# Hybrid encoder layer on one core: the convolution norm's means from split sums, its low parts one piece later, the ninth tile of values from a 64-wide operand, and the first weight load on ScalarE's queue

## The chip, the cores and the metric

One Trainium2 chip, one core. The metric is the time of one execution of the program in microseconds (us) on that core; smaller is better. The engines work side by side: TensorE (PE) multiplies matrices into PSUM, VectorE (DVE) and ScalarE (ACT) work element by element, GpSimd (POOL) does the same more slowly and issues some transfers, and SyncE (SP) issues most transfers (DMA).

## The reference

One layer of a streaming encoder in float32 for 1024 prompt frames and 32 frames of a running stream, 1056 rows (T) in all, D_MODEL 1024:

```python
p = x @ w_in                      # GLU pair | q | k | v | forget logits | branch gates
u = p[:, :512] * sigmoid(p[:, 512:1024])
y = conv_1d(u_ext, w_dw) + b_dw   # causal, depthwise, 31 taps, 512 channels
y = silu(layer_norm(y, ln_conv_g, ln_conv_b))      # norm over the 512 channels
y_conv = y @ w_conv_out
o = attention(q, k, v, cumsum(log_sigmoid(f)))     # 8 heads of 64, frame-causal
m = sigmoid(g_conv) * y_conv + sigmoid(g_attn) * (o @ w_attn_out)
x1 = layer_norm(alpha * x + m @ w_o)
x2 = layer_norm(alpha * x1 + relu(x1 @ w_up)**2 @ w_down)
```

Returned are x2, the new keys, values and forget logarithms, and the last convolution rows.

## The kernel before

Everything lies transposed: channels on the 128 partitions, frames along the free axis, in three chunks of 352 columns (`CH`). To keep float32 accuracy with the faster operand form fp32r, each operand is split in a high part (a copy to fp32r, made by ScalarE) and a low part (the operand minus the high part, made by VectorE), and a product is three products: high by high, high by low, low by high. `mm3` and `dense` write these; a group for eight row blocks of 128 has 24 products. A weight matrix comes in two halves (`W.load`), each of which is split (`W.split`) into `whi` and `wlo`.

The order of every engine's instructions is written out by the program: the class `Issue` keeps an estimated clock per engine, and background steps (generators) say with `yield` from when they may go on; `I.service()`, called between products, lets due steps issue. `yield (MARGIN, tiles)` means: not before these tiles have been ready for 3 us by that estimate. `I.flush()` issues all that is left of the background steps at once.

The first stage, in the order of TensorE's row:

- 19 warm-up products on constants (`keep_warm`), then the first GLU product (`glu`, kind b, tile 0, chunk 0), which takes its input as it comes: `x_stream` loads pieces `xr0`, `xr1`, ... of two row blocks each and the halves of the first weight matrices, and splits them. Between its products stand 5 and 2 more warm-up products.
- The other GLU products. Behind the third of tile 0 the background step `conv` begins: 31 multiply-adds on VectorE per channel tile (`ca0` to `ca3`).
- The values (`ps_v`): for two halves of the heads, nine tiles of frames. A tile is an operand of 128 frames against 260 columns of weights, 24 products. The ninth tile takes the last 128 frames, of which only the 32 of the running stream are used.
- q and k, then 16 tiles of branch gates (`gates`): three groups per tile, `g0_0`, `g0_1`, `g0_2`, `g1_0` and so on, each copied out of PSUM by ScalarE (`gt0_0`, ...) and stored. The first six tiles belong to this stage, where such products have eight PSUM buffers; then comes `I.flush()`. The other ten tiles fill gaps in the attention stage, where they have two buffers (`bbank`): `g6_2` needs the buffer of `g6_0`, hence the copy `gt6_0`.

Beside the gates the rest of `conv` runs, the norm over the 512 channels, in three column blocks of 362 (`CC`): `summed` adds the four channel tiles (`lns_m0`, ...); TensorE multiplies the sum with a matrix of 1/512 (`mean_c`), which gives the mean on all partitions (`ps_mu_c0`, ...), a float32 product; VectorE subtracts it, ScalarE squares, and the same gives the variance (`ps_var_c0`, ...); ScalarE takes the root and VectorE the reciprocal (`rstd_c0`, ...). Then twelve pieces (block c, tile j) follow. For a piece VectorE scales (here called y), ScalarE makes the sigmoid `csig`; one piece later VectorE multiplies with it (called z), ScalarE makes the high part `csh`, VectorE the low part `csl`, and both are stored. GpSimd clears buffers of the attention stage and issues the first head's loads when the memory of this stage is free.

Of the kernel before, what the change touches and what calls it, by code (L numbers as in the profile page):

```python
# [9 lines left out]
F32 = mybir.dt.float32  # L10
# [7 lines left out]
P = 128  # L18
# [249 lines left out]
def hybrid_layer(ctx: ExitStack, tc, io):  # L268
# [34 lines left out]
    act(tiny, eps, AF.Sigmoid)  # L303

    def par(name, j):
        return prm[:, PRM[name] + j:PRM[name] + j + 1]
# [17 lines left out]
    class Weights:  # L324
# [4 lines left out]
        def load(self):  # L329
            i = len(self.raw)  # L330
            held["raw"] += 1
            self.raw.append(ring.tile([P, RW // 2], F32, tag="raw", bufs=RAWB, name=f"raw{i}"))
            w = plan[i // 2]
            n = w.shape[1] // 2
            dma(self.raw[i][:, :n], w[:, i % 2 * n:(i % 2 + 1) * n])
# [157 lines left out]
    with pool("conv") as pv_, pool("a") as pa, pool("pa", space=PSUM) as psa:  # L493
# [6 lines left out]
        def x_stream():  # L500
            raw = []

            def issue():
                i = len(raw)
                if i < 4 * NCH:
                    r = pa.tile([P, 2, CH], F32, tag="xr", bufs=XB, name=f"xr{i}")
                    dma(r, io["x"][2 * (i % 4):2 * (i % 4) + 2, :, chunks[i // 4]].rearrange("k p t -> p k t"))
                    raw.append(r)

            W.load()  # L510
            issue()
            issue()
            W.load()
            for _ in range(XB - 2):
                issue()
                if len(raw) == 4:
                    W.load()
                    W.load()
            W.split()
            for i in range(4 * NCH):  # L520
                if i == 1:
                    W.split()
                    W.load()
                    W.load()
                yield [raw[i]]
                cs = chunks[i // 4]
                for n in range(2):
                    k = 2 * (i % 4) + n
                    act(xh[k][:, cs], raw[i][:, n, :], AF.Copy)
                    tt(xl[k][:, cs], raw[i][:, n, :], f32(xh[k][:, cs]), SUB)  # L530
                xin.append(i)
                for _ in range((0, 1, 1, 2)[i] if i < 4 else 1):
                    issue()
# [22 lines left out]
        mean_c = pv_.tile([P, P], F32, name="mean_c")  # L556
        nc.gpsimd.memset(mean_c, 1.0 / C_CONV)
# [26 lines left out]
        def glu(kind, j, c):  # L584
# [3 lines left out]
            if (kind, j, c) == ("b", 0, 0):  # L588

                terms = on_x(glu_w[kind, j], c)  # L590
                for k, (wh, _, h, l) in enumerate(terms):
                    mm(ps, wh, h, k == 0, False)
                    mm(ps, wh, l, False, False)
                    keep_warm({1: 5, 3: 2}.get(k, 0))
                    I.service()
# [17 lines left out]
        def conv():  # L613
# [11 lines left out]
            def summed(kind, c, src):  # L625
# [4 lines left out]
                return a  # L630
# [5 lines left out]
            for c in range(3):  # L636
                yield (MARGIN, [sums[c]])
                mu = bank(f"mu_c{c}")[:, :CC]
                mm(mu, mean_c, sums[c], True, True)
# [6 lines left out]
            for c in range(3):  # L646
                yield (MARGIN, [sums[c]])
                var = bank(f"var_c{c}")[:, :CC]
                mm(var, mean_c, sums[c], True, True)
# [6 lines left out]
            late = None  # L656
            for piece in pieces + [None]:
                yield ("dve", 1500)
                if piece:
# [4 lines left out]
                    act(sg, y, AF.Sigmoid, bias=par("lcb", j))  # L664
                if late:
# [3 lines left out]
                    act(hi, z, AF.Copy)  # L669
                    tt(lo, z, f32(hi), SUB)  # L670
# [70 lines left out]

        for half in range(2):
            ws = [W.take() for g in range(2)]
            for t in range(9):
                tk = slice(t * P, (t + 1) * P) if t < 8 else slice(T - P, T)
                ps = bank("v")[:, :VW]
                terms = []
                for k in range(KD):
                    wh, wl = (w[:, (k % 4) * VW:(k % 4 + 1) * VW] for w in ws[k // 4])
                    terms.append((xh[k][:, tk], xl[k][:, tk], wh, wl))  # L750
                dense(ps, terms)
                r = P if t < 8 else DEC
                ps = ps[P - r:P, :]
                v32 = pa.tile([P, 256], F32, tag="v32", bufs=2, name=f"v32_{half}_{t}")
                act(v32[:r], ps[:, 0:256], AF.Copy)
                act(zt[0:r, t, 4 * half:4 * half + 4], ps[:, 256:VW], AF.Copy)
# [1202 lines left out]
```

## Time and profile before

| | us |
|---|---|
| median of 3 runs | 1445.39 (1444.92 to 1445.43) |
| the profiled execution | 1445.13 |
| its span, first to last instruction | 1443.0 |
| TensorE busy | 1427.9 |
| VectorE busy | 1121.0 |
| ScalarE busy | 679.1 |

The profile is of one execution. A timeline row gives start, length, engine, source line, operation, output and inputs with shapes, and in brackets the idle time ahead of it and what ended it. Nearly all operations have the line of a helper, so tile names tell them apart, and the names come without numbers. Lengths of TensorE's products are those of one product through a pipeline and overlap; the pace is the distance of their starts.

### The profile page before, as it was taken

The page shows a single profiled execution, that of the slowest core. Times are in us where ns is not written, and L with a number is a line of the kernel's source. Part 1 is how long each engine was busy: PE and PEld are TensorE (multiplying, and loading weights), DVE is VectorE, ACT ScalarE, POOL GpSimd, SP SyncE. Part 2 cuts the span into 40 slices and gives each one's busy share as a digit, 9 for nine tenths or more (in the row PEclk, how much of TensorE's full clock was granted, in tenths as well). Part 3 has the DMA queues.
Part 4 walks back from the last instruction along what each step waited for, and adds up shares of the span by engine and source line. Part 5 has one row for each costly group of instructions (what it writes and reads, how often), then busy time and mean ns, then how long its engine had stood idle before and what let it go on. Part 6 is the DMA issues. An engine that isn't in the chain of part 4 may idle for free.

```text
span 1443.0 us, 28013 instructions
## 1 busy us (share of the span) xinstructions
PE 1427.9 (99%) x10643; PEld 1406.3 (97%) x10643; DVE 1121.0 (78%) x1927; ACT 679.1 (47%) x1426; POOL 124.5 (9%) x183
## 2 busy tenths in 40 slices
PE   9999999999999999999999999999999999999996
PEld 8999999999999999999999999999999999999996
DVE  6999899875666555756697888889876799889668
ACT  5113433455656556533245666676657323322134
POOL 0000000023455533000000000000000000000000
PEclk9999999999999999999999999999999999999998
DMA  7125454278455557425243348766689999894212
GB/s 247 48 61 160 159 171 167 85 244 233 120 150 147 155 146 260 152 93 182 85 138 120 131 152 295 249 241 230 228 283 342 340 321 330 270 324 179 67 45 77
DMA packets 157441, 267.91 MB, mean 186 GB/s; under 512 B 22680, under 2 KB 81272, under 8 KB 157308
## 3 DMA queue, kind: packets, MB, share of 16 engines
q1 hardware_dynamic: 156492, 264.24, 55.0%
q0 software_dynamic: 544, 1.59, 0.5%
q8 instruction: 84, 1.38, 0.4%
q14 instruction: 49, 0.40, 0.1%
q10 hardware_dynamic: 272, 0.29, 0.1%
HBM read 168.29 MB, written 97.74 MB: 184 GB/s over the span
## 4 chain that ended last, share of the span: by engine, by line
PE 97%; DVE 1%; ACT 0%; DMA 0%; issue 0%; SPq 0%; DVEq 0%
PE ps_u L206 18%; PE ps_d L206 17%; PE ps_g L206 13%; PE ps_o L206 6%; PE ps_dn L206 6%; PE ps_up L206 5%; PE ps_v L206 4%; PE ps_yc L206 3%; PE ps_k L206 3%; PE ps_glua L206 3%; PE ps_q L206 3%; PE ps_glub L206 3%; PE ps_yo L206 3%; PE ps_s L206 3%; PE ps_pv L206 2%; PE ps_tr L210 2%
## 5 line engine op out<-in xcount | busy, mean ns | idle before, releaser
L235 DVE SCALAR_TENSOR_TENSOR ca<-u,prm,ca 128x1086 f32<-128x1086 f32 x120 | 161.8, 1348 | 2.4
L206 PE MATMUL ps_g<-xh,whi 128*128 128x352 f32 x384 | 131.8, 343 | 0.0
L218 ACT ACTIVATE swhi<-s 128x512 fp32r<-128x512 f32 x100 | 61.9, 624 | 148.2 <-DVE s L227 139.8
L206 PE MATMUL ps_g<-xh,wlo 128*128 128x352 f32 x384 | 123.8, 322 | 0.0
L206 PE MATMUL ps_g<-xl,whi 128*128 128x352 f32 x384 | 121.5, 322 | 0.0
L206 PE MATMUL ps_u<-tl,swhi 128*128 128x264 f32 x416 | 118.4, 285 | 0.0
L206 PE MATMUL ps_u<-th,swhi 128*128 128x264 f32 x416 | 118.2, 284 | 0.0
L206 PE MATMUL ps_u<-th,swlo 128*128 128x264 f32 x416 | 118.2, 284 | 0.0
L218 ACT ACTIVATE whi<-raw 128x512 fp32r<-128x512 f32 (+1 forms) x120 | 69.7, 624 | 68.6 <-PE ps_glua L206 21.8
L227 DVE TENSOR_TENSOR tl<-ps_tr,th 128x512 fp32r<-128x512 f32 (+2 forms) x96 | 51.5, 553 | 60.1 <-ACT th L218 59.4
L206 PE MATMUL ps_d<-hu_h,swhi 128*128 128x264 f32 x480 | 93.0, 285 | 0.0
L206 PE MATMUL ps_d<-hu_l,swhi 128*128 128x264 f32 x480 | 92.8, 285 | 0.0
L218 ACT ACTIVATE r<-r 128x528 f32<-128x528 f32 (+1 forms) x120 | 73.9, 615 | 37.8 <-DVE r L227 35.5
L227 DVE TENSOR_TENSOR r<-r,ps_u 128x528 f32<-128x528 f32 x91 | 62.7, 701 | 29.5 <-PE ps_u L206 29.5
L227 DVE TENSOR_TENSOR wlo<-raw,whi 128x512 fp32r<-128x512 f32 (+1 forms) x100 | 64.9, 687 | 23.5 <-ACT whi L218 21.6
L206 PEld LDWEIGHTS ps_u<-th,swhi 128*128 128x128 f32 x416 | 78.3, 188 | 0.0
L206 PEld LDWEIGHTS ps_u<-th,swlo 128*128 128x128 f32 x416 | 78.3, 188 | 0.0
L206 PEld LDWEIGHTS ps_u<-tl,swhi 128*128 128x128 f32 x416 | 78.2, 188 | 0.0
L227 POOL TENSOR_TENSOR acc<-acc,lnrest 128x288 f32<-128x288 f32 x4 | 3.0, 796 | 856.7 <-ACT lnrest L218 856.7
L206 PEld LDWEIGHTS ps_d<-hu_h,swhi 128*128 128x128 f32 x480 | 74.6, 189 | 0.3 <-issue 0.2
L206 PEld LDWEIGHTS ps_d<-hu_l,swhi 128*128 128x128 f32 x480 | 74.6, 189 | 0.0
L206 PEld LDWEIGHTS ps_g<-xh,whi 128*128 128x128 f32 x384 | 72.7, 189 | 0.8
(424 smaller groups left out, 5005.5 us busy)
## 6 DMA issues: line engine op xcount, KB each, us to landing
h_s<-sp SPq DMA_DIRECT2D x84, 528.0 KB
raw<-in_w_in_dram SPq DMA_DIRECT2D x64, 256.0 KB
hu_h<-h_s SPq DMA_DIRECT2D x30, 528.0 KB
hu_l<-h_s SPq DMA_DIRECT2D x30, 528.0 KB
sraw<-in_w_up_dram SPq DMA_DIRECT2D x52, 256.0 KB
hu<-h_s SPq DMA_DIRECT2D x24, 528.0 KB
sraw<-in_w_ds_dram SPq DMA_DIRECT2D x48, 256.0 KB
g_s<-gt SPq DMA_DIRECT2D x48, 176.0 KB
```

Of the source, the lines that this page charges most:

```text
L206: self.nc.tensor.matmul(ps, lhsT=w, rhs=x, start=start, stop=stop)
L210: self.nc.tensor.transpose(ps, x, ident)
L218: self.nc.scalar.activation(out, in_, func, **kw)
L227: (self.nc.vector if eng == "dve" else self.nc.gpsimd).tensor_tensor(out, a, b, op)
L235: self.nc.vector.scalar_tensor_tensor(out, a, s, b, op0, op1)
```

## The change

Four edits. **(a)** `x_stream`: the first half of the first weight matrix is loaded through ScalarE's queue instead of SP's, and ScalarE's first table load and `tiny` stand behind that issue; the second half is split behind the second input piece instead of the first; the first GLU product has 2 and 1 warm-up products inside it instead of 5 and 2. **(b)** `summed` splits each sum of the norm in a high part (`csh_m0`, ...) and a low part (`csl_m0`, ...), `mean_c` is fp32r, and a mean is two fp32r products instead of one float32 product. **(c)** The low part of a piece and its stores are written one piece later, behind the next piece's z. **(d)** The ninth tile of values: ScalarE copies the 32 columns of each high and each low part side by side into `xs`, an operand 64 wide, which is multiplied with the high and the low weights, 16 products per half; rows 0 to 31 and 32 to 63 of the result are copied out and added by VectorE. (The product of the two low parts comes along; it was left out before.)

```diff
-    act(tiny, eps, AF.Sigmoid)
...
-        def load(self):
+        def load(self, queue=None):
...
-            dma(self.raw[i][:, :n], w[:, i % 2 * n:(i % 2 + 1) * n])
+            dma(self.raw[i][:, :n], w[:, i % 2 * n:(i % 2 + 1) * n], queue)
...
-            W.load()
+            W.load(nc.scalar)
+            act(tiny, eps, AF.Sigmoid)
...
-                if i == 1:
+                if i == 2:
                     W.split()
...
-        mean_c = pv_.tile([P, P], F32, name="mean_c")
-        nc.gpsimd.memset(mean_c, 1.0 / C_CONV)
+        mean_c = pv_.tile([P, P], F32R, name="mean_c")
+        nc.gpsimd.memset(f32(mean_c), 1.0 / C_CONV)
...
-                    keep_warm({1: 5, 3: 2}.get(k, 0))
+                    keep_warm({1: 2, 3: 1}.get(k, 0))
...
-                return a
+                parts = [pv_.tile([P, CC], F32R, tag=x, bufs=4, name=f"{x}_{kind}{c}") for x in ("csh", "csl")]
+                act(parts[0], a, AF.Copy)
+                tt(parts[1], a, f32(parts[0]), SUB)
+                return parts
...
-                yield (MARGIN, [sums[c]])
+                yield (MARGIN, sums[c])
...
-                mm(mu, mean_c, sums[c], True, True)
+                for i, a in enumerate(sums[c]):
+                    mm(mu, mean_c, a, i == 0, i == 1)
...
-                mm(var, mean_c, sums[c], True, True)
+                for i, a in enumerate(sums[c]):
+                    mm(var, mean_c, a, i == 0, i == 1)
...
-            late = None
-            for piece in pieces + [None]:
+            late = last = None
+            for piece in pieces + [None, None]:
...
+                before, last = last, None
...
                     act(hi, z, AF.Copy)
+                    last = c, j, z, hi, lo
+                if before:
+                    c, j, z, hi, lo = before
                     tt(lo, z, f32(hi), SUB)
...
+        xs = pa.tile([P, 2, CH], F32R, tag="xr", bufs=XB, name="xs").rearrange("p a x -> p (a x)")
+        xs = xs[:, :2 * KD * DEC].rearrange("p (k x) -> p k x", k=KD)
+        for k in range(KD):
+            for i, t in enumerate((xh, xl)):
+                act(xs[:, k, i * DEC:(i + 1) * DEC], f32(t[k][:, SEQ:T]), AF.Copy)
...
-                dense(ps, terms)
+                if t < 8:
+                    dense(ps, terms)
+                else:
+                    for n, (x, *w2) in enumerate(terms):
+                        for i, w in enumerate(w2):
+                            mm(ps[0:2 * DEC], x, w, n == i == 0, n == KD - 1 and i == 1)
+                        I.service()
...
+                    for i in range(2):
+                        act(both[i], ps[i * DEC:(i + 1) * DEC], AF.Copy)
+                    tt(both[0], both[0], both[1], ADD)
+                    ps = both[0]
```

The estimates of `Issue` move other instructions with these. In TensorE's row the first product of a mean goes from the middle of the group `g2_0` into `g2_2`, the last variance from `g3_0` into `g4_1`. The PSUM buffer of `g6_0` is one whose last reader was the copy `gt3_1`, and is now one whose last reader is `gt5_2`; `g6_2` waits for `gt6_0` in both. Behind the last piece the order of TensorE, VectorE and ScalarE is the same before and after.

ScalarE at the end of the first stage, before, from the copy of the stage's last gate product (`gt5_2`) to the copy of the next stage's first (`gt6_0`); the numbers in `csig2_3` are block and tile:

```order
L218 ACTIVATE gt5_2_3515<-ps_g5_2_94_3478 128x352
L218 ACTIVATE whi29_3518<-raw58_3250 128x512
L218 ACTIVATE whi29_3518<-raw59_3254 128x512
L218 ACTIVATE csig2_3_3529<-ca3_261,prm_131 128x362
L218 ACTIVATE csh2_2_3532<-ca2_260 128x362
L218 ACTIVATE csh2_3_3541<-ca3_261 128x362
L218 ACT_TABLE_LOAD
L218 ACTIVATE tiny_134<-eps_132 128x1
L218 ACTIVATE gt6_0_3617<-ps_g6_0_3592 128x352
```

The same place after the change, from `gt5_2` on; `csh2_2`, `csh2_3`, the table load, `tiny` and `gt6_0` come behind the last row shown:

```order
L218 ACTIVATE gt5_2_3503<-ps_g5_2_94_3468 128x352
L218 ACTIVATE whi29_3506<-raw58_3254 128x512
L218 ACTIVATE whi29_3506<-raw59_3258 128x512
L218 ACTIVATE csig1_3_3517<-ca3_261,prm_131 128x362
L218 ACTIVATE csh1_2_3520<-ca2_260 128x362
L218 ACTIVATE csig2_0_3527<-ca0_258,prm_131 128x362
L218 ACTIVATE csh1_3_3530<-ca3_261 128x362
L218 ACTIVATE csig2_1_3537<-ca1_259,prm_131 128x362
L218 ACTIVATE csh2_0_3540<-ca0_258 128x362
L218 ACTIVATE csig2_2_3547<-ca2_260,prm_131 128x362
L218 ACTIVATE csh2_1_3550<-ca1_259 128x362
L218 ACTIVATE csig2_3_3559<-ca3_261,prm_131 128x362
```

Behind `gt5_2` one sigmoid and two high parts stood ahead of `gt6_0`, and now five sigmoids and six high parts do.

VectorE from the split of weight matrix 29 (behind `gt5_2` in both) to the end of the norm, before:

```order
L227 TENSOR_TENSOR wlo29_3519<-raw58_3250,whi29_3518 128x512
L227 TENSOR_TENSOR wlo29_3519<-raw59_3254,whi29_3518 128x512
L235 SCALAR_TENSOR_TENSOR ca3_261<-ca3_261,prm_131,rstd_c2_3153 128x362
L235 SCALAR_TENSOR_TENSOR ca2_260<-ca2_260,prm_131,csig2_2_3486 128x362
L227 TENSOR_TENSOR csl2_2_3533<-ca2_260,csh2_2_3532 128x362
L235 SCALAR_TENSOR_TENSOR ca3_261<-ca3_261,prm_131,csig2_3_3529 128x362
L227 TENSOR_TENSOR csl2_3_3542<-ca3_261,csh2_3_3541 128x362
```

The same after the change, up to the low part of piece (1,3); behind it the operations of block 2 go on in the same turn, up to the low part of piece (2,3):

```order
L227 TENSOR_TENSOR wlo29_3507<-raw58_3254,whi29_3506 128x512
L227 TENSOR_TENSOR wlo29_3507<-raw59_3258,whi29_3506 128x512
L235 SCALAR_TENSOR_TENSOR ca3_261<-ca3_261,prm_131,rstd_c1_3233 128x362
L235 SCALAR_TENSOR_TENSOR ca2_260<-ca2_260,prm_131,csig1_2_3482 128x362
L227 TENSOR_TENSOR csl1_1_3486<-ca1_259,csh1_1_3485 128x362
L235 SCALAR_TENSOR_TENSOR ca0_258<-ca0_258,prm_131,rstd_c2_3298 128x362
L235 SCALAR_TENSOR_TENSOR ca3_261<-ca3_261,prm_131,csig1_3_3517 128x362
L227 TENSOR_TENSOR csl1_2_3521<-ca2_260,csh1_2_3520 128x362
L235 SCALAR_TENSOR_TENSOR ca1_259<-ca1_259,prm_131,rstd_c2_3298 128x362
L235 SCALAR_TENSOR_TENSOR ca0_258<-ca0_258,prm_131,csig2_0_3527 128x362
L227 TENSOR_TENSOR csl1_3_3531<-ca3_261,csh1_3_3530 128x362
```

The low part stands one piece later, and behind the weight's split begin the operations of piece (1,3) instead of (2,3).

ScalarE at the start of the program, before, up to the high part of the fourth row block:

```order
L218 ACT_TABLE_LOAD
L218 ACTIVATE tiny_134<-eps_132 128x1
L218 ACTIVATE whi0_210<-raw0_186 128x512
L218 ACTIVATE xh0_139<-xr0_188 128x352
L218 ACTIVATE xh1_140<-xr0_188 128x352
L218 ACTIVATE whi0_210<-raw1_192 128x512
L218 ACTIVATE xh2_141<-xr1_190 128x352
L218 ACTIVATE xh3_142<-xr1_190 128x352
```

The same after the change:

```order
L201 DMA raw0_185<-in_w_in_dram 128x512
L218 ACT_TABLE_LOAD
L218 ACTIVATE tiny_134<-eps_132 128x1
L218 ACTIVATE whi0_210<-raw0_185 128x512
L218 ACTIVATE xh0_138<-xr0_188 128x352
L218 ACTIVATE xh1_139<-xr0_188 128x352
L218 ACTIVATE xh2_140<-xr1_190 128x352
L218 ACTIVATE xh3_141<-xr1_190 128x352
L218 ACTIVATE whi0_210<-raw1_192 128x512
```

The load of `raw0` is issued here, and the split of `raw1` stands behind the two parts of `xr1`; VectorE's low parts follow the same order.

## Rows read from the trace of the kernel before

**Rows 1.** Parts 1 and 4 of the page, the whole span: busy time of an engine, its share of the span and its instructions; the last line is the chain of work that ended last, by engine.

```profile
PE 1427.9 (99%) x10643; PEld 1406.3 (97%) x10643; DVE 1121.0 (78%) x1927; ACT 679.1 (47%) x1426; POOL 124.5 (9%) x183
...
PE 97%; DVE 1%; ACT 0%; DMA 0%; issue 0%; SPq 0%; DVEq 0%
```

**Rows 2.** The chain that ended last, in order of time, between 240 and 340 us: start, length (us), engine, tile and number of instructions. `ps_g` are the gate products, `ps_mu_c` and `ps_var_c` the products with the matrix of means in the norm of the convolution.

```profile
245.34 24.91 PE ps_g L206 x156
270.25 0.61 PE ps_mu_c L206 x2
...
286.44 48.03 PE ps_g L206 x300
```

**Rows 3.** The same chain over the whole span: the product of the values (`ps_v`, 18 tiles of 24 products of 260 columns).

```profile
100.71 51.65 PE ps_v L206 x432
```

**Rows 4.** Timeline of VectorE (DVE) at the end of the norm of the convolution: start, length, instruction, and in brackets how long the engine had been idle before it and who released it. `csl` is the low part, `wlo` the low part of a weight matrix; the two SCALAR_TENSOR_TENSOR are the piece's scaling (written y in this text, its input is `rstd_c`) and the product with its sigmoid (written z, its input is `csig`).

```profile
313.28 0.54 DVE L227 TENSOR_TENSOR csl<-ca,csh 128x362 fp32r<-128x362 f32 x1 [0.62 <-ACT csh L218]
...
315.44 0.54 DVE L227 TENSOR_TENSOR csl<-ca,csh 128x362 fp32r<-128x362 f32 x1 [0.61 <-ACT csh L218]
...
319.14 1.30 DVE L227 TENSOR_TENSOR wlo<-raw,whi 128x512 fp32r<-128x512 f32 x2 [0.99 <-DMA g_s<-gt]
320.36 0.59 DVE L235 SCALAR_TENSOR_TENSOR ca<-ca,prm,rstd_c 128x362 f32<-128x362 f32 x1
320.86 0.59 DVE L235 SCALAR_TENSOR_TENSOR ca<-ca,prm,csig 128x362 f32<-128x362 f32 x1
322.07 0.54 DVE L227 TENSOR_TENSOR csl<-ca,csh 128x362 fp32r<-128x362 f32 x1 [0.61 <-ACT csh L218]
322.52 0.59 DVE L235 SCALAR_TENSOR_TENSOR ca<-ca,prm,csig 128x362 f32<-128x362 f32 x1
```

**Rows 5.** Timeline of ScalarE (ACT): one root of the norm, and then the stretch of rows 4. `gt` is the copy of a gate product out of PSUM; the one at 318.12 is `gt5_2`, the one at 325.08 `gt6_0`. `csh` is the high part of a piece, `whi` that of a weight matrix.

```profile
282.01 0.56 ACT L218 ACTIVATE rstd_c<-ps_var_c,eps 128x362 f32<-128x362 f32 x1
...
318.12 0.46 ACT L218 ACTIVATE gt<-ps_g 128x352 f32<-128x352 f32 x1 [0.54 <-PE ps_g L206]
318.49 1.15 ACT L218 ACTIVATE whi<-raw 128x512 fp32r<-128x512 f32 x2
321.54 0.49 ACT L218 ACTIVATE csh<-ca 128x362 fp32r<-128x362 f32 x1
323.15 0.51 ACT L218 ACTIVATE csh<-ca 128x362 fp32r<-128x362 f32 x1 [1.11 <-DVE ca L235]
323.67 1.28 ACT L218 ACT_TABLE_LOAD   x1
325.08 0.45 ACT L218 ACTIVATE gt<-ps_g 128x352 f32<-128x352 f32 x1
```

**Rows 6.** Timeline of TensorE (PE): the last product of the gate group `ps_g6_1`, and the first of `ps_g6_2` behind it.

```profile
325.39 0.32 PE L206 MATMUL ps_g<-xh,wlo 128*128 128x352 f32 x1
325.57 0.43 PE L206 MATMUL ps_g<-xh,whi 128*128 128x352 f32 x1
```

**Rows 7.** Timeline of VectorE in the norm of the convolution, from the first mean on: one column block's four subtractions, the start of its sum of squares, the next block's subtractions, later the three reciprocals and the first two pieces.

```profile
270.89 1.86 DVE L227 TENSOR_TENSOR ca<-ca,ps_mu_c 128x362 f32<-128x362 f32 x4 [0.15 <-PE ps_mu_c L206]
272.67 0.53 DVE L227 TENSOR_TENSOR lns_v<-sq_c,sq_c 128x362 f32<-128x362 f32 x1
274.39 1.85 DVE L227 TENSOR_TENSOR ca<-ca,ps_mu_c 128x362 f32<-128x362 f32 x4
...
284.69 6.96 DVE L239 RECIPROCAL rstd_c<-rstd_c 128x362 f32<-128x362 f32 x3
291.56 1.01 DVE L235 SCALAR_TENSOR_TENSOR ca<-ca,prm,rstd_c 128x362 f32<-128x362 f32 x2
```

**Rows 8.** Timeline of the first 11 us: TensorE's warm-up products (`ps_warm`, first 19, later 5 whose weight loads are shown), the split of the second half of the first weight matrix on ScalarE and VectorE with the idle time before it, and the six low parts of the input behind it on VectorE.

```profile
1.19 4.11 PE L542 MATMUL ps_warm<-warm 128*128 128x256 bf16 x19 [1.19 <-DVE warm L537]
...
6.88 0.44 PEld L542 LDWEIGHTS <-warm 128*128 128x128 bf16 x5
6.88 0.63 ACT L218 ACTIVATE whi<-raw 128x512 fp32r<-128x512 f32 x1 [0.93 <-DMA raw<-in_w_in_dram]
...
7.54 0.69 DVE L227 TENSOR_TENSOR wlo<-raw,whi 128x512 fp32r<-128x512 f32 x1 [0.98 <-ACT whi L218]
...
8.15 2.70 DVE L227 TENSOR_TENSOR xl<-xr,xh 128x352 fp32r<-128x352 f32 x6
```

**Rows 9.** Stretches at the start: from and to (us), length, busy us and instructions of each engine, then granted TensorE clock (1.00 is 2.4 GHz), DMA share and GB/s.

```profile
2.00:3.00 1.00, 1.00 (x7) 0.73 (x5) 0.00 (x0) 0.22 (x2) 0.00 (x0) 1.00 0.69 205
...
4.00:5.00 1.00, 1.00 (x6) 0.69 (x5) 0.40 (x1) 0.57 (x1) 0.00 (x0) 1.00 0.99 338
```

**Rows 10.** The same view at the end of the program, where TensorE has done its last product.

```profile
1430.00:1432.00 2.00, 1.70 (x7) 0.98 (x6) 0.63 (x3) 1.01 (x3) 0.40 (x1) 1.00 0.23 82
...
1434.00:1436.00 2.00, 0.00 (x0) 0.00 (x0) 1.97 (x3) 0.19 (x1) 0.65 (x1) 0.81 0.00 0
1436.00:1438.00 2.00, 0.00 (x0) 0.00 (x0) 2.00 (x7) 2.00 (x5) 0.00 (x0) 0.50 0.05 17
```

**Rows 11.** Timeline of GpSimd (POOL): it clears a buffer of the first head when the last variance product is done, then issues that head's loads (the last of them at 293.23).

```profile
286.56 1.00 POOL L827 MEMSET k<- 64x1088 f32 x1 [284.84 <-PE ps_var_c L206]
...
293.23 0.61 POOL L201 DMA_DIRECT2D q<-c_s  x1
```

More of the change, by code (lines that the diff above doesn't have):

```diff
@@ L646, in conv @@
             for c in range(3):
-                yield (MARGIN, [sums[c]])
+                yield (MARGIN, sums[c])
                 var = bank(f"var_c{c}")[:, :CC]
-                mm(var, mean_c, sums[c], True, True)
+                for i, a in enumerate(sums[c]):
+                    mm(var, mean_c, a, i == 0, i == 1)
                 rstds.append(pv_.tile([P, CC], F32, tag="lnrstd", bufs=3, name=f"rstd_c{c}"))
@@ L744, in hybrid_layer @@
             for t in range(9):
-                tk = slice(t * P, (t + 1) * P) if t < 8 else slice(T - P, T)
+                tk = slice(t * P, (t + 1) * P)
                 ps = bank("v")[:, :VW]
@@ L749, in hybrid_layer @@
                     wh, wl = (w[:, (k % 4) * VW:(k % 4 + 1) * VW] for w in ws[k // 4])
-                    terms.append((xh[k][:, tk], xl[k][:, tk], wh, wl))
-                dense(ps, terms)
+                    terms.append((xh[k][:, tk], xl[k][:, tk], wh, wl) if t < 8 else (xs[:, k, :], wh, wl))
                 r = P if t < 8 else DEC
-                ps = ps[P - r:P, :]
+                if t < 8:
[5 more added lines that the diff above has]
+                        I.service()
+                    both = pa.tile([P, 2, CH], F32, tag="xr", bufs=XB, name=f"xs_{half}")
+                    both = [both[:DEC, i, :VW] for i in range(2)]
+                    for i in range(2):
+                        act(both[i], ps[i * DEC:(i + 1) * DEC], AF.Copy)
+                    tt(both[0], both[0], both[1], ADD)
+                    ps = both[0]
                 v32 = pa.tile([P, 256], F32, tag="v32", bufs=2, name=f"v32_{half}_{t}")
-                act(v32[:r], ps[:, 0:256], AF.Copy)
-                act(zt[0:r, t, 4 * half:4 * half + 4], ps[:, 256:VW], AF.Copy)
+                act(v32[:r], ps[0:r, 0:256], AF.Copy)
+                act(zt[0:r, t, 4 * half:4 * half + 4], ps[0:r, 256:VW], AF.Copy)
                 vs = pa.tile([P, 4, P], F32R, tag="vs", bufs=2, name=f"vs_{half}_{t}")
```

## Prediction

> **What bounds the kernel now.** I read the page first: TensorE is busy for 99% of the span, and the chain that ended last is 97% TensorE [rows 1]. So an edit gains what it takes off TensorE's row of products, and loses what TensorE has to wait for. Next I read the chain in order of time around the norm of the convolution, to see what each product with the means costs there [rows 2], and the product of the values [rows 3]. Then I looked for the places where TensorE has no slack against the other engines. One stands right behind the norm. The third gate product behind the stage, `g6_2`, needs the PSUM buffer that ScalarE empties with the copy `gt6_0`, since the attention stage has two buffers for such products. That copy stands on ScalarE behind the whole rest of the norm: the last high part, a table load, then `gt6_0`, done at 325.53 [rows 5]. TensorE's last product of `g6_1` starts at 325.39 and the first of `g6_2` at 325.57 [rows 6], 0.18 us later, where the products of this stretch follow each other every 0.16 us (48.03 us for 300, rows 2). TensorE arrives there within 0.02 us of the moment when the buffer comes free. Any lengthening of the norm's tail behind `gt5_2` is therefore paid by TensorE in full.
>
> **Means as two fp32r products.** Before, each of six products takes 0.61 us from the row [rows 2]: 3.66 us. After, there are twelve fp32r products of 362 columns; the trace has the form with 352 columns at 0.160 [rows 2], so 0.165 each, 12 × 0.165 = 1.98. That gives back 1.7 us. Bounds: 0.16 each makes it 1.75; if each change of operand form cost another 0.05, 1.4. The six splits add six copies on ScalarE and six subtractions on VectorE, which has 22% of its time free [rows 1]; they hide, except for what they do to the tail, below.
>
> **Ninth tile in two products.** Two halves lose 24 − 16 = 8 products each. 51.65 us for 432 [rows 3] is 0.120 per product, so 16 × 0.120 = 1.9 us. The stationary operand is now 64 wide instead of 128; no row shows that form. If it made the remaining 32 products half as long, 32 × 0.06 = 1.9 more would come back; if the gain were eaten by something in that form, 0. I take 1.9, because the moving columns stay 260 and these set the pace in rows 3. ScalarE's 16 small copies ahead and four more copies behind lie beside products with eight PSUM buffers to spare; without that cover they would cost some 3 us.
>
> **First load by ScalarE, its second half one piece later, four warm-up products fewer.** TensorE is waiting for data in the first 11 us. What holds it is VectorE's row of low parts: it idles 0.98 us for the second half of the first weight matrix, which ScalarE idles 0.93 us for, and only then come the weight's low part and six input parts, 2.70 us long [rows 8]. In the new order the two input parts stand first, and their data are on the same queue ahead of that half (256 KB, at 338 GB/s [rows 9] about 0.75 us earlier). So most of the 0.98 us of idle time goes; I take 0.5, from 0 (later input pieces arrive no sooner) to 0.98. The load's issue on ScalarE I count at nothing: from 4 us on the transfers run at 338 GB/s with the DMA engines 0.99 busy, and only the stretch from 2 to 3 us has room (205 GB/s) [rows 9]. The Trainium skill, "DMA: Bandwidth & Descriptors", section on issuing engines, says that spreading transfers over issuing engines gives no bandwidth, only issue time; the busy share in rows 9 agrees, and by that rule the sum stays as it is. If a second queue did fill the room from 2 to 3 us (338 − 205 GB/s, 133 KB), all data would come up to 0.4 us earlier and the sum would be 1446.1. The warm-up products removed lie in TensorE's waits, so they count zero.
>
> **Low parts one piece later, and where the whole norm goes.** The edit removes VectorE's wait of 0.61 us per piece [rows 4]; a piece then takes its three operations, 0.50 + 0.51 + 0.45 = 1.46 us, instead of 2.16 (315.44 − 313.28). That alone shortens the tail. But the splits of the sums put each mean product later in TensorE's row: the first from the third gate tile's first group to its third, the last variance from the first group of the fourth tile into the second group of the fifth. So more of the norm is left when TensorE issues its last product ahead of the attention stage, and ScalarE's order shows it: behind `gt5_2` stood one piece's sigmoid and two high parts, now five sigmoids and six high parts, all ahead of the table load and `gt6_0`.
>
> Count from the start of the copy `gt5_2`. Now: VectorE splits the weight, starts y at +2.24 (320.36 − 318.12), and `gt6_0` ends at +7.41 (325.53 − 318.12) [rows 4, 5]. After the change y also starts at +2.24, but of piece (1,3), with four more pieces behind it. Five rounds of three operations at 1.46 bring VectorE to the last z at +9.55 (ScalarE needs about 1.1 per piece, so it keeps up). From the start of that z to the end of `gt6_0` it takes 325.53 − 322.52 = 3.01 now [rows 4, 5], so `gt6_0` ends at +12.55.
>
> TensorE has two groups of 24 products between, 48 × 0.160 = 7.7 us. And there is a second, smaller wait: the buffer of `g6_0` itself is now one that `gt5_2` empties (before, one that was free long ahead), so `g6_0` waits for that copy too. Both together: lag of `gt5_2` behind TensorE's last product of that group, plus 12.55, minus 7.7. For the lag I added up both engines from the first mean on. TensorE: 234 gate products × 0.160 + 12 × 0.165 = 39.4 us to the end of `g5_2`. VectorE: three blocks of 3.5 us (274.39 − 270.89, rows 7) plus 1.15 each for the new split (0.61 of wait and 0.54 of work, as a low part now has in rows 4), 14.0; three weight splits 3.7; the reciprocals 6.9 [rows 7]; eighteen piece operations at 0.49, 8.8; a wait of some 3.6 ahead of the third weight split, because ScalarE has a high part, a table load of 1.28, two roots and three gate copies to do first [rows 5]; about 2.5 of smaller waits and starts. That is 39.5, and ScalarE reaches `gt5_2` 0.2 to 1.5 us behind TensorE; I take 0.6. The new wait is 0.6 + 12.55 − 7.7 = 5.5 us, of which 4.4 stand in one piece ahead of `g6_2`. Bounds 4.9 and 7 (upper: stores of the pieces queue on SP behind two weight loads and a gate load, and a buffer of high parts comes free late).
>
> Behind this VectorE and ScalarE have the attention's first products to serve, and the order there is unchanged, so the 5.5 us are not won back. The first head's loads wait for the last variance product [rows 11], which comes about 13 us later; they are needed at 286.44 + 48.03 = 334.5 [rows 2], 41 us after the last issue at 293.23, so they stay hidden.
>
> **The sum.** −1.7 − 1.9 − 0.5 + 5.5 = +1.4 us. The profiled execution took 1445.13, 0.26 below the median of the runs shown: 1445.13 + 1.4 = **1446.5**. The forecast's own range is 1445.2 to 1448.8.
>
> **Rivals.** (1) The clock falls in the new wait: slower. At the end of the program TensorE is done at 1431.7 (1.70 us of work in that stretch), and the granted clock goes from 1.00 to 0.50 inside 1434 to 1436, where its mean is 0.81, so at 1435.2: 3.5 us after the last product [rows 10]. The wait ahead of `g6_2` is 4.4. [...] Price: at the start 19 warm-up products take 4.11 us, 0.216 each, where five later ones follow each other every 0.11 [rows 8]; so TensorE runs at the low level (1.2 GHz) for at least 4.1 us and loses 2.1. Time: 1446.5 + 2.1 = 1448.6. The Trainium skill, "TensorE: Matmul & The Clock Gate", Part 1, has the half-rate clock as the default that returns once TensorE is idle and is lifted by sustained work; rows 8 and 10 agree, and by that rule the sum is 1448.6 instead of 1446.5.
>
> (2) The tail does not hold TensorE: ScalarE and VectorE run further ahead than my count, or the rounds overlap better, so that `gt6_0` is as early as now. For it speaks that the change removes 0.61 us of wait per piece; against it the order of ScalarE, in which sixteen piece operations of VectorE lie between the weight split and `gt6_0`. Time: 1445.13 − 4.1 = 1441.0.
>
> (3) With four warm-up products fewer the clock rises later at the start, or falls again in the waits between the first products: a loss as in (1), 1448.6. Against it: the 19 products ahead are untouched and the gaps are under 1 us.
>
> **How the numbers follow.** About what a measurement of this kernel can tell from no change is 0.2%, 2.9 us: from 1442.5 to 1448.3. Chances: forecast 0.56 (0.03 of it slower, the rest within); clock falls 0.28 (0.04 within, 0.24 slower); tail doesn't hold 0.09 (faster); start clock 0.04 and late buffers beyond my bound 0.03 (slower). That makes faster 0.09, same 0.57, slower 0.34. The range leaves out most of (2) and the worst of (1): 1442.8 to 1450.0.
>
> **What would show it.** TensorE idle ahead of `g6_2`, released by ScalarE's `gt`: 4.4 us if right, none if (2). Ahead of `g6_0` about 1 us. `gt6_0` ending 12.5 us after `gt5_2` starts. Mean products 0.33 a pair; 432 − 16 = 416 products of values, in 49.7 us. VectorE's waits for `csh` gone in the pieces. Granted clock below 1.00 for a few us behind the wait would show (1), below 1.00 or products at 0.31 us after 8 us would show (3). Wrong altogether I would be if `g6_2` waited for nothing: then the change is a plain gain of 4 us.

## The result and the profile after

The changed kernel takes 1450.4 us, the median of 7 runs (1449.47 to 1451.03), against 1445.43 us for the kernel before (7 runs, 1444.92 to 1445.86): 1.0032 times the time, 95% interval 1.0022 to 1.0041. It is slower by more than the 0.2% that was taken as the bound, and 0.4 us above the range. The profiled execution took 1449.47 us with a span of 1447.2, so the pair of profiles differs by 4.2 us of span.

What each edit takes off TensorE came back as forecast. The chain that ended last, of the changed kernel (start, length, engine, tile, instructions):

```profile
12.22 3.85 PE ps_glua L206 x24
...
100.34 49.71 PE ps_v L206 x416
...
274.64 0.33 PE ps_mu_c L206 x2
...
327.07 10.47 PE ps_g L206 x54
...
657.94 47.20 PE ps_o L206 x390
...
1432.62 1.47 PE ps_md_last L206 x6
```

and the rows of the same view of the kernel before that stand against the first and the last two:

```profile
12.60 3.85 PE ps_glua L206 x24
...
654.59 47.20 PE ps_o L206 x390
...
1429.27 1.47 PE ps_md_last L206 x6
```

The start is 0.38 us earlier, the values take 49.71 instead of 51.65 us [rows 3], and a mean takes 0.33 instead of 0.61 [rows 2]. The loss stands in one place. TensorE's timeline behind the norm of the convolution, with the idle time in brackets:

```profile
313.78 0.32 PE L206 MATMUL ps_g<-xh,wlo 128*128 128x352 f32 x1
315.02 0.43 PE L206 MATMUL ps_g<-xh,whi 128*128 128x352 f32 x1 [0.92 <-ACT gt L218]
...
322.60 0.32 PE L206 MATMUL ps_g<-xh,wlo 128*128 128x352 f32 x1
327.07 0.43 PE L206 MATMUL ps_g<-xh,whi 128*128 128x352 f32 x1 [4.15 <-ACT gt L218]
...
328.14 0.39 PE L206 MATMUL ps_g<-xh,whi 128*128 128x352 f32 x1
328.34 0.49 PE L206 MATMUL ps_g<-xl,whi 128*128 128x352 f32 x1
328.63 0.49 PE L206 MATMUL ps_g<-xh,wlo 128*128 128x352 f32 x1
```

These are the two waits of the forecast: `g6_0` at 315.02, `g6_2` at 327.07, where the kernel before had none [rows 6]. From 328.3 us on the products follow each other every 0.29 us instead of 0.16. The granted clock of the same stretch (from and to, length, busy us and instructions of PE, PEld, DVE, ACT and POOL, granted clock, DMA share, GB/s):

```profile
327.00:328.00 1.00, 0.93 (x6) 0.93 (x7) 0.00 (x0) 0.37 (x2) 0.88 (x4) 1.00 0.58 175
328.00:329.00 1.00, 1.00 (x6) 1.00 (x6) 0.00 (x0) 0.00 (x0) 0.00 (x0) 0.63 0.58 174
329.00:330.00 1.00, 1.00 (x5) 1.00 (x4) 0.00 (x0) 0.00 (x0) 0.00 (x0) 0.50 0.60 176
330.00:331.00 1.00, 1.00 (x6) 1.00 (x5) 0.00 (x0) 0.00 (x0) 0.00 (x0) 0.50 1.00 85
331.00:332.00 1.00, 1.00 (x6) 1.00 (x6) 0.00 (x0) 0.00 (x0) 0.00 (x0) 0.67 0.65 66
332.00:333.00 1.00, 1.00 (x8) 1.00 (x7) 0.00 (x0) 0.00 (x0) 0.00 (x0) 1.00 0.80 277
```

So the clock went to its low level (1.2 GHz) for some 3.4 us, 1.2 us after TensorE had taken up work again. The 54 products of that stretch take 10.47 us; at 0.160 they would take 8.64: 1.83 us lost.

Who holds `g6_2` shows in ScalarE's timeline; `gt5_2` is the copy at 314.52, `gt6_0` and `gt6_1` are the two at 326.57, `gt6_2` the one at 334.98:

```profile
314.52 0.45 ACT L218 ACTIVATE gt<-ps_g 128x352 f32<-128x352 f32 x1
...
324.64 0.51 ACT L218 ACTIVATE csh<-ca 128x362 fp32r<-128x362 f32 x1 [0.31 <-DVE ca L235]
325.17 1.28 ACT L218 ACT_TABLE_LOAD   x1
...
326.57 0.80 ACT L218 ACTIVATE gt<-ps_g 128x352 f32<-128x352 f32 x2
334.98 0.47 ACT L218 ACTIVATE gt<-ps_g 128x352 f32<-128x352 f32 x1 [7.61 <-DMA g_s<-gt]
```

and ScalarE follows VectorE, whose pieces come in rounds of 1.46 us (318.19 − 316.73) up to the last z at 324.02:

```profile
316.73 0.59 DVE L235 SCALAR_TENSOR_TENSOR ca<-ca,prm,rstd_c 128x362 f32<-128x362 f32 x1
...
318.19 0.59 DVE L235 SCALAR_TENSOR_TENSOR ca<-ca,prm,rstd_c 128x362 f32<-128x362 f32 x1
...
324.02 0.59 DVE L235 SCALAR_TENSOR_TENSOR ca<-ca,prm,csig 128x362 f32<-128x362 f32 x1
```

The last row of ScalarE points at something the forecast had not looked at: `gt6_2` waits 7.61 us for the landing of `gt6_0`'s store, since the attention stage has two buffers for such copies. The kernel before has that wait too, 6.02 us long; in neither does TensorE wait for it. The experiments come back to it. The row of the kernel before:

```profile
332.24 0.47 ACT L218 ACTIVATE gt<-ps_g 128x352 f32<-128x352 f32 x1 [6.02 <-DMA g_s<-gt]
```

Why so much of the norm is left behind `gt5_2`: VectorE's reciprocals, with which the pieces begin, start at 295.18 instead of 284.69 [rows 7]. The six splits stand in VectorE's row, each with a wait of 0.57 to 0.63 us for the high part; its last low part of a sum is ready at 290.60, and then it idles 3.37 us for the split of a weight. TensorE's last product with the means comes at 295.38, 4.8 us behind its operand, since the planner asks for 3000 ns by its own count. VectorE's timeline there:

```profile
290.06 0.54 DVE L227 TENSOR_TENSOR csl_v<-lns_v,csh_v 128x362 fp32r<-128x362 f32 x1 [0.57 <-ACT csh_v L218]
293.97 1.29 DVE L227 TENSOR_TENSOR wlo<-raw,whi 128x512 fp32r<-128x512 f32 x2 [3.37 <-ACT whi L218]
295.18 6.96 DVE L239 RECIPROCAL rstd_c<-rstd_c 128x362 f32<-128x362 f32 x3
```

### The profile page after: what moved, and what is told of

Its sections match the earlier page's. It is cut to its first block, busy times and chain, and to the rows that moved or that the text cites. A ratio compares the mean times of both kernels' runs of the same rounds, so it can differ in the third digit from the quotient of the medians.

```text
span 1447.2 us, 28010 instructions
## 1 busy us (share of the span) xinstructions
PE 1425.8 (99%) x10623; PEld 1405.3 (97%) x10623; DVE 1122.8 (78%) x1935; ACT 685.5 (47%) x1452; POOL 124.2 (9%) x183
## 4 chain that ended last, share of the span: by engine, by line
PE 96%; DVE 2%; DMA 1%; ACT 1%; issue 0%; SPq 0%; DVEq 0%
PE ps_u L206 18%; PE ps_d L206 17%; PE ps_g L206 12%; PE ps_o L206 6%; PE ps_dn L206 6%; PE ps_up L206 5%; PE ps_v L206 3%; PE ps_yc L206 3%; PE ps_k L206 3%; PE ps_glua L206 3%; PE ps_q L206 3%; PE ps_glub L206 3%; PE ps_yo L206 3%; PE ps_s L206 3%; PE ps_pv L206 2%; PE ps_tr L210 2%
```

## The experiments

All were timed beside the kernel before on the same chip (its medians there are 1445.47 to 1445.74). The table has, from each trace, TensorE's waits for a gate copy (gt), the stretch with the low clock, the first product of the attention's scores, the first product of the up projection's long stage (`ps_u`), that of the last norm (`ps_md_last`) and what lies from there to the end of the span (to 0.05 us, as the span is read to 0.1), and the median and ratio of the timed runs.

| kernel | waits for gt | low clock | scores | ps_u | md_last | to the end | median us | ratio (95%) |
|---|---|---|---|---|---|---|---|---|
| before | none | none | 334.31 | 820.75 | 1429.11 | 13.89 | 1445.43 | |
| after | 0.92, 4.15 | 328 to 332 | 337.38 | 824.09 | 1432.46 | 14.74 | 1450.40 | 1.0032 (1.0022–1.0041) |
| e1_no_means | none | none | 329.85 | 818.83 | 1428.15 | 13.95 | 1444.13 | 0.9989 (0.998–0.9997) |
| e2_only_means | 1.52, 7.67 | 329 to 339 | 344.79 | 831.20 | 1439.73 | 13.87 | 1456.43 | 1.0071 (1.0057–1.0085) |
| e3_margin500 | 0.65, 2.53 | 334 to 341 | 336.34 | 826.41 | 1434.84 | 14.96 | 1449.42 | 1.0024 (1.0015–1.0033) |
| e4_busy | 0.55, 1.43, 0.75 | none | 337.33 | 824.26 | 1432.61 | 14.89 | 1449.92 | 1.0025 (1.0014–1.0035) |
| e5_margin_queue | 1.97 | none | 332.79 | 819.47 | 1428.09 | 14.91 | 1445.53 | 1.0001 (0.9992–1.001) |
| e6_busy_queue | 0.56, 1.25 | none | 336.33 | 822.80 | 1432.09 | 14.61 | 1447.97 | 1.0017 (1.0008–1.0026) |
| e7_start_ninth | 0.78 | none | 333.15 | 821.13 | 1429.51 | 13.89 | 1445.65 | 0.9999 (0.999–1.0007) |
| e8_only_late | none | none | 330.72 | 824.70 | 1433.16 | 14.24 | 1450.95 | 1.0036 (1.0022–1.005) |
| e9_pool_queue | none | none | 330.33 | 816.86 | 1425.21 | 13.89 | 1441.54 | 0.997 (0.996–0.9981) |
| e10_pool | none | none | 330.73 | 818.64 | 1428.72 | 13.88 | 1441.17 | 0.997 (0.9958–0.9981) |
| e11_margin1000 | 2.10, 2.72 | 334 to 341 | 336.64 | 825.12 | 1433.49 | 15.41 | 1448.62 | 1.0019 (1.001–1.0028) |

**Which edit makes the waits.** In e1 the means are fp32 products of whole sums again, in the changed kernel (`mean_c` is float32 again too; the products with `var` change in the same way):

```diff
-                parts = [pv_.tile([P, CC], F32R, tag=x, bufs=4, name=f"{x}_{kind}{c}") for x in ("csh", "csl")]
-                act(parts[0], a, AF.Copy)
-                tt(parts[1], a, f32(parts[0]), SUB)
-                return parts
+                return [a]
...
-                for i, a in enumerate(sums[c]):
-                    mm(mu, mean_c, a, i == 0, i == 1)
+                mm(mu, mean_c, sums[c][0], True, True)
```

> The changed kernel with the means of the norm as fp32 products of whole sums again (the start, the late low parts and the ninth tile stay). Theory T (the sums' split pushes the last variance product, and with it the norm's tail, behind gt5_2): ScalarE's order now has no piece of the norm between gt5_2 and gt6_0, so TensorE waits for nothing ahead of g6_0 and g6_2 and the granted clock stays 1.00 around 330 us; 1445.4 - 0.4 (start) - 1.9 (ninth tile) = 1443.1 us. Rival R (the extra round of the low parts and the stores that it shifts on SP hold TensorE): the waits of 0.9 and 4.1 us stay, the time is 1450.4 + 1.7 = 1452.

In e2 this edit stands alone in the kernel before.

> The kernel before with the split sums and fp32r means alone. Theory T: the same five sigmoids and six high parts stand between gt5_2 and gt6_0, and each piece takes 2.16 us instead of 1.46, so the tail is some 3.5 us longer than in the changed kernel and the wait ahead of g6_2 is 7 to 8 us; with the fall of the clock (1.8) and the 1.7 us that the means give back the time is 1445.4 - 1.7 + 9 + 1.8 = 1454.5 us. Rival R: no wait, the means give back 1.7 us: 1443.7.

Both went by theory T: no wait and a clock of 1.00 in e1, two waits in e2, TensorE's timeline:

```profile
317.80 0.43 PE L206 MATMUL ps_g<-xh,whi 128*128 128x352 f32 x1 [1.52 <-ACT gt L218]
333.38 0.66 PE L206 MATMUL ps_g<-xh,whi 128*128 128x352 f32 x1 [7.67 <-ACT gt L218]
```

So the split sums make the wait. The three other edits together shorten it by 4.1 us (9.19 against 5.07). Most of that is the low parts one piece later: from `gt5_2` to `gt6_0` it takes 15.58 us in e2 (317.30 to 332.88) and 12.05 in the changed kernel, 3.5 less, which is five rounds of 1.46 instead of 2.16 us. The rival, that the late low parts hold TensorE, fell. e2 came out 1.9 us above what was expected; its 54 products behind the wait take 11.57 us instead of 8.64, 2.9 us lost to the clock where 1.8 were put in. e1 gained 1.5 us of the expected 2.3 (1444.13 against 1445.64 for the kernel before beside it): its lead over the kernel before is 2.5 us at the output projection (651.89 against 654.43), 1.9 at `ps_u` and 1.0 at `ps_md_last`. In between TensorE waits 0.4 us for a low part of the output projection's weights and 0.7 for a sum (`ps_d <- ACT acc`), waits that the kernel before doesn't have: TensorE has no slack at those later places either.

**Whether work taken off TensorE comes back at all.** e7 has the new start and the ninth tile alone.

> The kernel before with the new start and the ninth tile in two products alone; both take work off TensorE ahead of the norm (0.4 and 1.9 us). Theory T (the end of gt6_0 is set by VectorE and ScalarE, not by TensorE): VectorE's chain is as late as before, TensorE reaches g6_2 about 2 us earlier and waits there 1.5 to 2.8 us: 1445 us, no gain that can be told. Rival R3 (what is taken off TensorE comes back in full): no wait, 1445.4 - 2.3 = 1443.1.

No gain, as T said, but not all by its way: the wait ahead of `g6_2` is 0.78 us, so the first scores come 1.16 us earlier than before. Half of that lead is left at the output projection (653.87 against 654.43) and none at `ps_u` (821.13 against 820.75); in between TensorE waits 0.7 us for `wlo_wo`, the low part of the output projection's weights. e7 is T by its time and between T and R3 by its trace.

e8 has the late low parts alone.

> The kernel before with the low parts one piece later alone. It takes nothing off TensorE. Theory T: nothing of the norm is left between gt5_2 and gt6_0, TensorE waits for nothing there, as before: 1445.4 us, the same. Rival R (the late low parts and their stores are what holds TensorE): waits for gt, 1447 or more.

Neither theory holds. TensorE waits for no gt, and the kernel is 5.5 us slower. With the shorter norm the planner counts the first scores as ready sooner: 510 gate products stand ahead of them in its order instead of 534. The 24 others (3.84 us) fill less well inside the attention: from the first scores to the first `ps_yc` it takes 221.24 us (551.96 − 330.72) instead of 213.90, 3.5 more than the 24 products, and the list of TensorE's waits has there, among others:

```profile
PE ps_tr L210 <- DVE tl L227: 2.2, 3, 1.6
...
PE ps_tr L210 <- DVE p L231: 0.5, 1, 0.5
PE ps_str L210 <- ACT ob L218: 0.5, 1, 0.5
```

Behind the changed kernel's own loss this does not stand: it has 534 products ahead of the scores, as before, and takes 214.13 us for the same stretch.

**Whether the clock fell for want of work.** e4 puts idle work in the wait of the changed kernel:

```diff
+                    if hook and (m, c) == (GA, 2):
+                        hook.pop()()
...
+        def busy():
+            ps = psb.tile([P, 512], F32, tag="tr", bufs=2, name="ps_busy")[:, :256]
+            for _ in range(32):
+                nc.tensor.matmul(ps, lhsT=bfs[:, :P], rhs=bfs[:, :256], start=True, stop=True)
```

> The changed kernel with 32 bf16 products of 256 columns, whose result nobody reads, ahead of g6_2: some 3.5 us of work in the wait of 4.1. Theory T (the clock falls because TensorE is idle): the wait shrinks to about 0.6 us, g6_2 starts at the same time, the granted clock stays 1.00 and the 54 products behind take 8.6 instead of 10.5 us: 1450.4 - 1.8 = 1448.6. Rival (the clock falls for another reason): g6_2's products stay at 0.29 us for 3.4 us, 1450.4.

The clock stayed at 1.00, so it had fallen because TensorE was idle: the mean granted clock of the span is 0.997 or 0.998 in all eight timed executions, and 0.994 to 0.996 in the seven of the changed kernel. The median is 0.5 us lower and not 1.8, and in the profiles the first scores come at the same time (337.33 against 337.38), since the next wait came up. TensorE's timeline, with one row of the granted clock behind the wait:

```profile
322.47 3.67 PE L975 MATMUL ps_busy<-bfs 128*128 128x256 bf16 x32
327.57 0.43 PE L206 MATMUL ps_g<-xh,whi 128*128 128x352 f32 x1 [1.43 <-ACT gt L218]
...
336.25 0.43 PE L206 MATMUL ps_g<-xh,whi 128*128 128x352 f32 x1 [0.75 <-ACT gt L218]
```

```profile
329.00:330.00 1.00, 1.00 (x8) 1.00 (x7) 0.00 (x0) 0.00 (x0) 0.00 (x0) 1.00 0.59 175
```

`gt6_0` came 0.5 us later than in the changed kernel, and at 336.25 `g7_1` waits for `gt6_2`, which waits for the store of `gt6_0`. The slow clock had covered that.

**Moving the means forward.** e3 asks a smaller distance of the planner, in both loops (means and variances):

```diff
-                yield (MARGIN, sums[c])
+                yield (500.0, sums[c])
```

> The changed kernel in which the planner asks 500 ns instead of 3000 between a ready sum and its product with the means. Theory T: the last variance product comes some 18 gate products earlier, one sigmoid and two high parts are left between gt5_2 and gt6_0 as in the kernel before, the waits are gone, and all three gains are kept: 1445.4 - 1.7 - 1.9 - 0.4 = 1441.4 us; granted clock 1.00 around 330 us. Rival R: the waits stay, 1450. A third way: the products with the means now stand so early that TensorE waits for their operands, some tenths of a us each.

The first wait went down from 4.15 to 0.65 us, the third way cost 0.67 (`ps_var_c <- ACT csh_v`), and the time stayed within the noise (1.0024 against 1.0032 times the kernel before). ScalarE's timeline, `gt6_0` and `gt6_2`:

```profile
323.45 0.80 ACT L218 ACTIVATE gt<-ps_g 128x352 f32<-128x352 f32 x2
333.90 0.47 ACT L218 ACTIVATE gt<-ps_g 128x352 f32<-128x352 f32 x1 [9.64 <-DMA g_s<-gt]
```

the store on SP's queue, behind the stores of the norm's pieces:

```profile
326.81 0.98 SPq L201 DMA_DIRECT2D g_s<-gt  x2
```

and TensorE, with the granted clock behind the wait:

```profile
334.42 0.66 PE L206 MATMUL ps_g<-xh,whi 128*128 128x352 f32 x1 [2.53 <-ACT gt L218]
```

```profile
336.00:338.00 2.00, 2.00 (x10) 1.91 (x10) 0.59 (x2) 0.46 (x2) 1.53 (x2) 0.50 0.99 244
338.00:340.00 2.00, 2.00 (x9) 1.69 (x8) 0.48 (x3) 0.56 (x2) 0.00 (x0) 0.50 1.08 281
```

`gt6_0` is done 1.6 us earlier than before, but SP issues its store at 326.81, as before (326.87), and it lands 7 us later. TensorE is now early enough to meet this second place without slack. e5, e6 and e11 test that, with a margin of 1000 ns (e5, e11), and gate tile 6 stored by ScalarE's queue (e5, e6):

```diff
-                dma(g_s[m, :, chunks[c]], g)
+                dma(g_s[m, :, chunks[c]], g, nc.scalar if m == GA else None)
```

> The changed kernel with a margin of 1000 ns ahead of the six products with the means, and the three stores of the gate tile 6 on ScalarE's queue instead of SP's. In the run with 500 ns the tail was short, but ScalarE then waited 9.64 us for the landing of gt6_0's store, issued 3.3 us after the copy and landed 7 us later, and TensorE 2.53 us for gt6_2 with the clock falling behind it. Theory T2 (that store, queued on SP behind the stores of the norm's pieces, is the second place without slack): the store leaves right behind gt6_0, TensorE waits for no gt, the granted clock stays 1.00; first scores at 334.5 - 4.0 = 330.5 to 331 us, end at 1445.4 - 4.0 = 1441.4, or up to 1.4 more if the seams behind 650 us take as much as in the run without the split means. Rival R2 (the transfers themselves are late, since the DMA engines are full): the wait stays 2 us or more, the time above 1446.

> The run with 32 idle products ahead of g6_2, and the stores of gate tile 6 on ScalarE's queue. There the clock stayed at 1.00, but 0.75 us of the 1.8 went into a third wait, for gt6_2, and 0.5 into a later gt6_0. T2: the third wait is gone: 1449.9 - 0.75 = 1449.2, and up to 0.5 less where gt6_0 is not late: 1448.7. R2: 1449.9 and the third wait still there.

> The changed kernel with the margin of 1000 ns alone, stores on SP's queue. It stands against the run with the same margin and ScalarE's queue (1445.5): T2: TensorE waits some 2 us for gt6_0 and then 1 to 2 us more for gt6_2, with a fall of the clock behind one of them: 1447.5 to 1449.5. R2 (the queue is of no account): 1445.5.

The wait for `gt6_2` is gone in e5 and e6 and 2.72 us in e11. e11 and e5 differ by the queue alone: 3.1 us of the median, 5.4 us at `ps_md_last` in the profiles, which are the wait and the fall of the clock behind it. The timed executions of e3 and e11 spread over 4 us (1447.62 to 1451.82 and 1446.70 to 1450.99) and the profiled ones were among the longest, so a fall of this length is not shown for all of them. R2 is out. e6 came out 0.7 us below its expectation. e5 still waits 1.97 us for `gt6_0`, which T2 had not expected, so it is no faster than the kernel before.

**Taking the split off VectorE.** What holds `gt6_0` in e5 is VectorE's row, by theory T. e9 and e10 move the six subtractions:

```diff
-                tt(parts[1], a, f32(parts[0]), SUB)
+                tt(parts[1], a, f32(parts[0]), SUB, "pool")
```

> The run with the margin of 1000 ns and ScalarE's queue for the stores of gate tile 6, and the six subtractions of the sums' splits on GpSimd instead of VectorE. There VectorE waits 0.57 us for each high part of a sum and takes 0.54 for the low part; without both its row in front of the pieces is up to 6.7 us shorter, and one high part is left between gt5_2 and gt6_0. Theory T (VectorE's row sets gt6_0): gt6_0 comes before TensorE is there at about 322 us, no wait for gt, clock 1.00, first scores at about 330.4: 1441.4 us, or up to 1.5 more where later seams take from it, as without the split means. Rival R4 (GpSimd's subtraction is so slow that the means come later): the wait of 2 us stays, 1445.

> The same with the stores of gate tile 6 on SP's queue. T2 (a store on SP waits behind the pieces' stores): with the short tail gt6_0 and its store are earlier too, so what is left of a wait for gt6_2 is under 1 us: 1441.4 to 1443. If the wait for the store's landing is as long as with the margin of 500 ns (9.64 us on ScalarE, 2.5 on TensorE), 1446 and more.

Both hold by T: no wait for gt, the clock stays, and the whole of the forecast's 4 us of gains arrives: 1441.54 and 1441.17 us, 0.3% below the kernel before. ScalarE's timeline of e10, from the one high part that is left to `gt6_2`:

```profile
318.18 0.51 ACT L218 ACTIVATE csh<-ca 128x362 fp32r<-128x362 f32 x1 [1.35 <-DVE ca L235]
318.71 1.28 ACT L218 ACT_TABLE_LOAD   x1
...
320.11 0.45 ACT L218 ACTIVATE gt<-ps_g 128x352 f32<-128x352 f32 x1
322.22 0.47 ACT L218 ACTIVATE gt<-ps_g 128x352 f32<-128x352 f32 x1 [1.66 <-PE ps_g L206]
329.15 0.46 ACT L218 ACTIVATE gt<-ps_g 128x352 f32<-128x352 f32 x1 [6.46 <-DMA g_s<-gt]
```

`gt6_0` is done at 320.56, ahead of TensorE, which ends `g6_1` at 322.2, and its store is early too, so SP's queue does no harm. Both runs also have the margin of 1000 ns; the subtractions on GpSimd with the margin of 3000 ns were not run, so what each of the two gives by itself is known for the margin alone (e11, 1448.62). e10's profiled execution, from which its row of the table is, was its longest (1444.54; the other five are 1440.86 to 1442.05); it lost time behind 650 us.

## Why the prediction was wrong

**Right, step by step.** The means −1.7 (measured 6 × (0.61 − 0.33) = 1.68), the ninth tile −1.9 (1.94), the start −0.5 (0.38; no run separates the queue from the later split, and the second queue did not fill the room from 2 to 3 us: 123 GB/s there, 205 before [rows 9]). The place and the mechanism of the loss: waits of 1 and 4.4 us ahead of `g6_0` and `g6_2` were forecast, 0.92 and 4.15 measured. The tail was counted to end 12.55 us behind the start of `gt5_2`; `gt6_0` started at 12.05 (326.57 − 314.52), and TensorE went on at 12.55. Rounds of 1.46 us and the last z at +9.55 (9.50) came as counted. The last variance product came 9.6 us later and not 13 (295.55 against 285.98), which entered no term. e1 and e2 show that the split of the sums makes this wait, e9 and e10 that it goes when the tail does.

**The step that failed** is the falling clock: the sum put it at nothing. The prediction read a fall 3.5 us after the last product at the end of the program [rows 10], set the wait of 4.4 us beside it, and still gave the fall half the chance of the forecast and left its 2.1 us out. It fell, behind 4.15 us of waiting. e3 and e11 show falls behind waits of 2.53 and 2.72 us, so the one row at the end was a poor measure of it. Its price was near: 2.1 forecast, 1.83 measured. It was read from the pace of the warm-up products, 0.216 us each [rows 8]; the granted clock of rows 9 says 1.00 in that stretch, which the prediction passed over. The Trainium skill, "TensorE: Matmul & The Clock Gate", Part 1, which the prediction weighed beside that row, has the clock come down once TensorE is idle; the traces agree, and 1448.6 was the better number.

The clock is not the whole miss. 1448.6 is still 1.8 us short of 1450.4. And in e4, where the clock stays up, the first scores come 3.02 us later than in the kernel before and not 1.4: a later `gt6_0` costs 0.5 us of it and the wait for `gt6_2` 0.75, for which the sum had nothing.

**The account of the pair of profiles.** Gains 1.68 + 1.94 + 0.38 = 4.00; waits 5.07; clock 1.83; together +2.9, where the first scores come 3.07 us later. By the distance of starts the account closes: `g6_2` begins 1.50 us later (327.07 against 325.57 [rows 6]), which is −4.00 and 5.50 of waiting, as forecast; from there to the first scores it takes 10.31 us instead of 8.74, 1.57 for the clock (less than the 1.83, since this stretch takes more than 54 × 0.160 in the kernel before too). Another 0.28 us go between there and the output projection (3.35 later at 657.94), in no one place. The last 0.85 us is behind TensorE's last work: from `ps_md_last` to the end of the span it takes 13.89 us in the profile before and 14.74 in that after. Up to the last piece of the chain both take 9.6 us (1438.70 − 1429.11 and 1442.04 − 1432.46), so it stands behind that, where only the last stores are left. The table shows values from 13.87 to 15.41, and 13.89 both for the kernel before and for e9, which has all four edits, so the four edits alone don't make it; as each kernel has one profile, it is not shown that it belongs to the execution. Sum +4.2. That the medians of the timed runs (4.97) are 0.8 us further apart than the spans stays open; the profiled execution was the shortest of the seven.

**What was not in the forecast.** The second place without slack, the store of `gt6_0`. The prediction named stores that queue on SP only as a bound of the tail. In the changed kernel it cost nothing, because the slow clock covered it; it decided e3, e4 and e11. And one sentence of the prediction does not hold as it stands: that an edit gains what it takes off TensorE's row. e7 takes 2.3 us off and gains nothing: 1.1 of it goes at `g6_2`, and the 1.2 us of lead at the scores are lost again by `ps_u`.

**Still open:** why the planner's order of e8 fills the attention so much worse than that of e1, which has 522 gate products ahead of the scores and does not lose there.

## What to carry to other kernels

Where one engine is busy for 99% and another place has no slack, work taken off the busy engine is worth only what the chain behind that place allows; shorten that chain first (here by six small subtractions on GpSimd, busy for 9% of the span [rows 1], and a smaller distance in the planner, 9 us between 1450.4 and 1441.2). A new wait of a few us on TensorE is to be priced with the fall of the clock behind it as the likely case. When one wait is removed, the next may stand behind it, covered by the first: look at the idle time of the engines off the path (ScalarE's 7.61 us for a store) before counting the gain.

## What the runs showed of the hardware

The clock's fall did not simply grow with the wait. Behind 4.15 us of waiting TensorE had the low level for 3.4 us, 1.2 us after it had begun to work again; behind waits of 2.53 and 2.72 us (e3, e11) it had it from 334 to 341 us, beginning just ahead of the first product; in the wait of 7.67 us (e2) from 329 to 339 us, beginning 4 us ahead of the first product. Waits of 1.97 and 2.10 us left the clock at 1.00 (e5, and the first wait of e11).

A store of 176 KB took 7 us from issue to landing in e3 (326.81 to 333.8), with the DMA engines 0.67 to 1.02 busy meanwhile, and its issue came 2.9 us after the copy was done (323.9), behind twelve stores of pieces and two loads that SP issued from 319.9 us on. Issued by ScalarE's queue (e5, at 325.06) it no longer held `gt6_2`, which came at 328.18, 4.6 us behind `gt6_0`, released by TensorE. The Trainium skill, "DMA: Bandwidth & Descriptors", section on issuing engines, has a second issuing engine save issue time and give no bandwidth; the earlier issue agrees with it, and why the landing is earlier by more than that no run here separates.

A subtraction of 128x362 took mostly 0.98 us on GpSimd (e9) and 0.54 on VectorE (the changed kernel); off VectorE's row it was worth it all the same.
